# Sums of squares for the first norm from the transposed tiles of x, and x in rows loaded later

## The chip, the cores and the metric

One core of a Trainium2 chip. The metric is the device time of one execution in microseconds (us). Engines: PE is TensorE (matrix products), ACT is ScalarE, DVE is VectorE, POOL is GpSimd, SP is SyncE, which here only issues loads. An engine works off its own instructions in order; engines wait for one another through semaphores.

## What is computed

Two transformer blocks on 256 tokens of width 2048, in float32. What matters here is the very start, the norm of the input and the first projection:

```python
def rms_norm(x, gain):
    xf = x.astype(jnp.float32)
    y = xf * lax.rsqrt(jnp.mean(xf * xf, axis=-1, keepdims=True) + EPS)
    return (y * gain.astype(jnp.float32)).astype(x.dtype)

def hybrid_mixer(xn, w_in, lb, hgrn_onorm, attn_qnorm, attn_knorm, w_out):
    proj = xn @ w_in
...
h = h + hybrid_mixer(rms_norm(h, norm_mix[l]), w_in[l], ...)
```

The mean over a token's 2048 features is a factor of the token alone. So the kernel multiplies x times gain with the weights at once and applies the factor, called `rstd`, when a product leaves PSUM.

## The kernel before

Everything runs on one core, in float32 products of three terms: each operand is split into a high part `hi` (ACT, line 392 for weights, 1379 for x) and a low part `lo` (DVE, lines 393 and 1380), and PE adds hi x hi, hi x lo and lo x hi (lines 443 to 445). Weights come in chunks of 512 KB into four buffers `raw` (SP, line 382); a chunk holds one or two feature tiles of 128 rows for a block of 512 output columns. There are four buffers each of `hi` and `lo`, so that splits run at most four chunks ahead of PE, and a load waits until DVE has split the chunk four places before.

The first two blocks, called c0 and c1 in the code, share the sixteen feature tiles of x transposed. These arrive with the chunks of weights into two regions `r` (line 1369, from an array that the host transposed) and are split by `first_split` into `xT`. The order of chunks at the start is written out by hand: features 0, 1, 2, 3, (4,5), (6,7) in turns for c0 and c1, then (8,9), (10,11), (12,13), (14,15) of c0, and then the same four of c1. A chunk of two tiles is 12 matmuls of 128x512 on PE.

x in rows, the tile `X`, is needed for two things. The residual add at the mixer's end reads it, and so does the sum of squares: `build_ss` (line 308) has ACT square a 128x512 piece with an accumulator (`junk`, the sums go to `ss`), and `make_rstd` adds the four partial sums, scales them and takes the reciprocal root by `rsqrt` (line 246): two integer steps on DVE (`rg`) and twelve small steps on POOL (`rh`, `rstd`). `X` is loaded in four column pieces of 512 KB from POOL's queue, each held back by a copy of eight columns (`gate`) from the low part of feature 5, 7, 9 or 11 (`X_GATES`). `prep` then spreads `rstd` over a row: DVE copies it wide into `wA`, PE transposes twice into `sdA`, DVE copies the result into `rstd_bc` (lines 635 to 647). Then POOL loads a table (`levels`).

What comes when on each engine is set by a planner inside the code. Chunks are emitted in the order above; between two chunks the side work, kept as generators in six lanes, takes a step if a lane's clock says that its data are there. `wait_for` and `mark` carry those estimates. The planner's costs set the order of instructions, and the chip then runs them with real semaphores.

Of the kernel before, what the change touches and what calls it, by code (L numbers as in the profile page):

```python
# [12 lines left out]
F32 = mybir.dt.float32  # L13
# [4 lines left out]
AF = mybir.ActivationFunctionType  # L18
ALU = mybir.AluOpType
# [3 lines left out]
P = 128  # L23
T = 256
D = 2048
KT = D // P
# [3 lines left out]
EPS = 1e-6  # L30
# [16 lines left out]
FIRST_SINGLE = 4  # L47
FIRST_LEN = 10
TURNS = 6
X_GATES = (5, 7, 9, 11)  # L50
WARM_UP = 10
BEHIND = 2.0

# [33 lines left out]
def block_kernel(ctx: ExitStack, tc: "_tile.TileContext", a: dict, out: bass.AP, phases=ALL_PHASES):  # L87
    nc = tc.nc
    ctx.enter_context(tc.manual_schedule())

    const = ctx.enter_context(tc.tile_pool(name="const", bufs=1))
# [7 lines left out]
    ready = {}  # L99
    uid = [0]  # L100

    def nm(s):
        uid[0] += 1
        return f"{s}_{uid[0]}"

    def wt(lane, dtype=F32):
        return tmp.tile([P, 512], dtype, tag=f"w{lane}", bufs={"B": 2, "E": 4, "A": 6}[lane], name=nm(f"w{lane}"))

    def st(role, n=8, dtype=F32):
        return small.tile([P, n], dtype, tag=role, name=nm(role))  # L110

    def sd(lane):
        return ps_side.tile([P, 512], F32, tag=f"sd{lane}", name=nm(f"sd{lane}"))

    def region(i, shape, dtype=F32):
        return reg.tile(shape, dtype, tag=f"r{i}", name=nm(f"r{i}"))
# [5 lines left out]
    clock = {"pe": 0.0, "act": 0.0, "dve": 0.0, "pool": 0.0}  # L122
    names = ("E", "B", "C", "D", "H", "A")
    lanes = {k: deque() for k in names}
# [20 lines left out]
    class Paced:  # L145
# [26 lines left out]
    pe, sca, vec, gps = (  # L172
        Paced(t, e) for t, e in ((nc.tensor, "pe"), (nc.scalar, "act"), (nc.vector, "dve"), (nc.gpsimd, "pool")))

    def mark(key):
        lane = now["lane"]
        ready.setdefault(key, done[lane] if lane is not None else 0.0)
# [37 lines left out]
    def wait_for(*keys):  # L215
        while any(k not in ready for k in keys) or (
            not now["forced"] and max(ready[k] for k in keys) > clock["pe"]
        ):
            yield WAIT
        lane = now["lane"]  # L220
        done[lane] = max([done[lane]] + [ready[k] for k in keys])
        last_on[lane] = None
# [14 lines left out]
    def load_x(c0, c1):  # L237
        nc.gpsimd.dma_start(out=X[:, :, c0:c1], in_=a["x"][:, c0:c1].rearrange("(t p) c -> p t c", p=P))
# [3 lines left out]
    def gcol(i):  # L242
        return gT[:, i : i + 1]


    def rsqrt(lane, x, n, mul=1.0, out=None):

        g = st(f"rg{lane}", n, I32)
        vec.tensor_scalar(g, x.bitcast(I32), 1, None, op0=ALU.logical_shift_right)
        vec.tensor_scalar(g, g, -1, RSQRT_MAGIC, op0=ALU.mult, op1=ALU.add)  # L250
        y = st(f"ry{lane}", n) if out is None else out
        h = st(f"rh{lane}", n)
        for i in range(3):
            y0 = g.bitcast(F32) if i == 0 else y
            m = mul if i == 2 else 1.0
            gps.tensor_tensor(h, y0, y0, op=ALU.mult)
            gps.tensor_tensor(h, h, x, op=ALU.mult)
            gps.tensor_scalar(h, h, -0.5 * m, 1.5 * m, op0=ALU.mult, op1=ALU.add)
            gps.tensor_tensor(y, h, y0, op=ALU.mult)
        return y  # L260

    rstd = {}
    rstd_sq = {}

    def make_rstd(lane, key, ss, want_sq=False):

        v = vec
        m = st(f"mr{lane}", 2)
        v.tensor_reduce(m, ss.rearrange("p (t c) -> p t c", t=2), axis=AX.X, op=ALU.add)
        ms = const.tile([P, 2], F32, name=nm("ms"))  # L270
        v.tensor_scalar(ms, m, 1.0 / D, EPS, op0=ALU.mult, op1=ALU.add)
        if want_sq:
            r2 = const.tile([P, 2], F32, name=nm("rsq"))
            v.reciprocal(r2, ms)
            rstd_sq[key] = r2
        else:
            rstd[key] = rsqrt(lane, ms, 2, out=const.tile([P, 2], F32, name=nm("rstd")))
        mark(("rstd", key))
# [3 lines left out]
    def parts_of(ver, kt):  # L282

        xT = xTs[0 if ver in ("mlp1", "mlp2") else 1]
        return xT[:, kt, 0, :], xT[:, kt, 1, :], xT[:, kt, :, :].rearrange("p x t -> p (x t)")
# [22 lines left out]
    def build_ss(ver, cb, want_sq):  # L308
        yield from wait_for(("x", ver, cb))
        if ver not in ss_tiles:  # L310
            ss_tiles[ver] = const.tile([P, 8], F32, name=nm("ss"))
        ss = ss_tiles[ver]
        for tt in range(2):
            junk = tmp.tile([P, 512], BF16, tag="junk", bufs=1, name=nm("junk"))
            sca.activation(
                junk, X[:, tt, cb * 512 : (cb + 1) * 512], AF.Square,
                accum_out=ss[:, tt * 4 + cb : tt * 4 + cb + 1],
            )
        yield
        if cb == 3:  # L320
            make_rstd("D", ver, ss, want_sq)
            yield
# [7 lines left out]
    acts = {k: Act() for k in ("mix", "cross", "mlp1", "na", "mlp2")}  # L330
# [57 lines left out]
    def emit_split(c):  # L388
        n = len(c.kts) * c.block.width
        c.hi = stream.tile([P, 1024], F32R, tag="hi", name=nm("hi"))  # L390
        c.lo = stream.tile([P, 1024], F32R, tag="lo", name=nm("lo"))
        nc.scalar.activation(c.hi[:, :n], c.raw[:, :n], AF.Copy)  # L392
        nc.vector.tensor_tensor(c.lo[:, :n], c.raw[:, :n], c.hi[:, :n], op=ALU.subtract)  # L393
        clock["act"] = max(clock["act"], clock["pe"] - 2.6) + 0.1 + n * 0.00083
        clock["dve"] = max(clock["dve"], clock["act"] + HOP) + 0.1 + n * 0.00104
        c.ready = clock["dve"]
# [966 lines left out]
    p0 = order[0]  # L1363
    xr = [region(i, [P, 8, T]) for i in (6, 7)]
# [9 lines left out]
    def first_split(kt):  # L1374

        act = acts[p0]
        act.put(kt, *parts_of(p0, kt))
        (hi, lo, _), src, g = act.parts_of[kt], xr[kt // 8][:, kt % 8, :], gcol(gains_of[p0] + kt)
        nc.scalar.activation(hi, src, AF.Copy, scale=g)
        nc.vector.scalar_tensor_tensor(lo, src, g, hi.bitcast(F32), op0=ALU.mult, op1=ALU.subtract)  # L1380
        mark(("act", id(act), kt))

    starters = {
        "mix": mixer, "cross": cross, "mlp1": lambda: mlp("mlp1", a["w_up"], a["w_down"]),
# [1 line left out]
    }  # L1386
    for p_ in order:
        starters[p_]()

    n = len(plan)  # L1390
    dma_i = split_i = 0
# [16 lines left out]
    def split(c):  # L1408
        if c.block.act is acts[p0]:
            for kt in c.kts:  # L1410
                if kt not in made:
                    made.add(kt)
                    first_split(kt)
                    if kt in X_GATES:
                        cb = X_GATES.index(kt)
                        gate = st("gate", 8)
                        nc.gpsimd.tensor_copy(gate, acts[p0].parts[kt][1][:, :8].bitcast(F32))
                        load_x(cb * 512, cb * 512 + 512)
                        ready["x", p0, cb] = clock["pe"] + 10.0
                        lanes["D"].append(build_ss(p0, cb, p0 in ("mlp1", "mlp2")))  # L1420
        emit_split(c)

    while dma_i < RAW_BUFS:
# [2 lines left out]
    while split_i < 2:  # L1426
        split(plan[split_i])
        split_i += 1
    for i in range(n):
        while dma_i < min(n, i + DMA_AHEAD):  # L1430
            while split_i <= dma_i - RAW_BUFS:
                split(plan[split_i])
                split_i += 1
            dma(plan[dma_i])
            dma_i += 1
        while split_i < min(n, i + 1 + SPLIT_AHEAD):
            split(plan[split_i])
            split_i += 1
        emit_mm(plan[i])
        step_all()  # L1440
# [69 lines left out]
```

## Time and profile before

| | us |
|---|---|
| median of 3 runs | 2430.24 (2428.49 to 2430.58) |
| the profiled execution | 2430.18 |
| its span, first to last instruction | 2428.4 |
| PE busy | 2419.5 |
| DVE busy | 1498.1 |
| ACT busy | 1183.2 |
| POOL busy | 183.6 |

The span is that of the profiled execution; 1.8 us of its time lie around the span. All positions in the text are microseconds from the span's start. "Granted clock" is TensorE's clock as a share of full speed. A row of the timeline with "x2" merges two instructions that follow each other, and its duration is that of both together. A float32 product of two plain operands leaves two records on PE.

### The profile page before, as it was taken

Reading aid. Unit: us, or ns where it says so; the run is one execution under the profiler, and the core shown is the slowest. Engines: PE = TensorE matmul, PEld = TensorE weight load, DVE = VectorE, ACT = ScalarE, POOL = GpSimd, SP = SyncE. Lnnn points to the kernel's source line nnn. Section 1 sums busy time; section 2 is a strip of 40 time slices with the busy share of each in tenths; the row PEclk is TensorE's granted clock in tenths of the full one; section 3 lists DMA queues with packets and bytes.
Section 4 is the critical chain, followed back from the end, with each engine's and each line's share of the span. In section 5 each row is a group of like instructions: output and inputs, shape, how many; then the busy total and the mean of one; then the engine's idle time right before and its main releaser. Section 6 shows DMA issues by size and latency. Waiting matters only on the chain.

```text
span 2428.4 us, 32811 instructions
## 1 busy us (share of the span) xinstructions
PE 2419.5 (100%) x12664; PEld 2073.9 (85%) x12664; DVE 1498.1 (62%) x1859; ACT 1183.2 (49%) x1608; POOL 183.6 (8%) x362
## 2 busy tenths in 40 slices
PE   9999999999999999999999999999999999999999
PEld 7979988888888888888888888888888888888887
DVE  6567666666665655565555666776655555655565
ACT  6455544465654444444445454554654444444442
POOL 1021012221000000000000412230000000000000
PEclk9999999999999999999999999999999999999999
DMA  8655444754555655565665655565555665656564
GB/s 283 195 170 170 138 141 158 241 184 157 182 192 190 192 189 188 193 198 184 191 192 181 203 173 179 174 194 177 173 193 185 196 195 187 195 186 192 189 200 164
DMA packets 127292, 453.33 MB, mean 187 GB/s; under 512 B 14608, under 2 KB 15376, under 8 KB 127136
## 3 DMA queue, kind: packets, MB, share of 16 engines
q1 hardware_dynamic: 122688, 439.87, 56.3%
q0 software_dynamic: 3584, 10.00, 1.4%
q8 instruction: 99, 1.62, 0.3%
q10 hardware_dynamic: 864, 1.38, 0.2%
q14 instruction: 57, 0.47, 0.1%
HBM read 449.02 MB, written 2.10 MB: 186 GB/s over the span
## 4 chain that ended last, share of the span: by engine, by line
PE 99%; DMA 0%; DVE 0%; ACT 0%; SPq 0%; issue 0%; ACTq 0%; DVEq 0%
PE acc L424 20%; PE acc L443 20%; PE acc L444 20%; PE acc L445 20%; PE acc L427 10%; PE acc L436 4%; PE sdA L168 3%; PE sdE L168 2%; DMA raw<-in_w_in_dram 0%; DVE lo L393 0%; ACT hi L392 0%; ACT r L168 0%; SPq L1369 0%; DVE X L168 0%; DVE lb L168 0%
## 5 line engine op out<-in xcount | busy, mean ns | idle before, releaser
L393 DVE TENSOR_TENSOR lo<-raw,hi 128x1024 fp32r<-128x1024 f32 (+1 forms) x838 | 1008.8, 1218 | 332.1 <-ACT hi L392 329.4
L392 ACT ACTIVATE hi<-raw 128x1024 fp32r<-128x1024 f32 (+1 forms) x838 | 869.6, 1052 | 552.8 <-PE acc L445 403.5
L424 PE MATMUL acc<-xT,hi 128*128 128x512 f32 (+1 forms) x2176 | 750.7, 391 | 0.0
L427 PE MATMUL acc<-xT,lo 128*128 128x256 f32 (+1 forms) x2176 | 606.2, 279 | 0.0
L443 PE MATMUL acc<-hi,r 128*128 128x512 f32 (+1 forms) x1408 | 543.4, 386 | 0.7 <-ACT r L168 0.7
L445 PE MATMUL acc<-hi,r 128*128 128x512 f32 (+1 forms) x1408 | 541.3, 384 | 0.0
L444 PE MATMUL acc<-lo,r 128*128 128x512 f32 (+1 forms) x1408 | 541.2, 384 | 0.0
L424 PEld LDWEIGHTS acc<-xT,hi 128*128 128x128 f32 x2176 | 408.4, 188 | 88.1
L427 PEld LDWEIGHTS acc<-xT,lo 128*128 128x128 f32 x2176 | 409.7, 188 | 0.6
L445 PEld LDWEIGHTS acc<-hi,r 128*128 128x128 f32 x1408 | 264.5, 188 | 53.1 <-DVE r L168 0.4
L443 PEld LDWEIGHTS acc<-hi,r 128*128 128x128 f32 x1408 | 264.6, 188 | 52.9 <-ACT r L168 1.1
L444 PEld LDWEIGHTS acc<-lo,r 128*128 128x128 f32 x1408 | 264.6, 188 | 51.2
L443 PE MATMUL acc<-hi,xT 128*128 128x512 f32 x736 | 291.6, 396 | 1.2 <-ACT hi L392 1.2
L444 PE MATMUL acc<-lo,xT 128*128 128x512 f32 x736 | 287.7, 391 | 0.8 <-DVE lo L393 0.8
L445 PE MATMUL acc<-hi,xT 128*128 128x512 f32 x736 | 287.2, 390 | 0.0
L168 DVE TENSOR_TENSOR wE<-acc,wE 128x256 f32<-128x256 f32 (+1 forms) x136 | 51.9, 421 | 220.3 <-ACT wE L168 220.2
L168 DVE SCALAR_TENSOR_TENSOR X<-acc,rsq,X 128x512 f32<-128x512 f32 x128 | 96.1, 751 | 147.6 <-PE acc L445 147.6
L168 ACT ACTIVATE wE<-acc 128x256 f32<-128x256 f32 (+1 forms) x136 | 49.3, 381 | 277.3 <-PE acc L427 277.3
L443 PEld LDWEIGHTS acc<-hi,xT 128*128 128x128 f32 x736 | 138.6, 188 | 31.4 <-issue 2.7
L445 PEld LDWEIGHTS acc<-hi,xT 128*128 128x128 f32 x736 | 138.6, 188 | 29.2
L444 PEld LDWEIGHTS acc<-lo,xT 128*128 128x128 f32 x736 | 138.8, 189 | 28.5 <-DVE lo L393 1.5
L436 PE MATMUL acc<-xT,hi 128*128 128x256 f32 (+1 forms) x544 | 100.1, 286 | 0.0
(188 smaller groups left out, 1397.2 us busy)
## 6 DMA issues: line engine op xcount, KB each, us to landing
raw<-in_mlp_w_dram SPq DMA_DIRECT2D x256, 512.0 KB, 4.4
raw<-in_w_up_dram SPq DMA_DIRECT2D x128, 512.0 KB, 4.5
raw<-in_w_down_dram SPq DMA_DIRECT2D x128, 512.0 KB, 4.3
raw<-in_w_in_dram SPq DMA_DIRECT2D x108, 512.0 KB, 3.7
raw<-in_na_w_qkv_dram SPq DMA_DIRECT2D x96, 512.0 KB, 3.7
raw<-in_w_out_dram SPq DMA_DIRECT2D x32, 512.0 KB, 4.3
raw<-in_na_w_o_dram SPq DMA_DIRECT2D x32, 512.0 KB, 3.7
raw<-in_w_iq_dram SPq DMA_DIRECT2D x16, 512.0 KB, 4.8
```

Source lines behind the costliest of these rows:

```text
L168: return f(*args, **kw)
L392: nc.scalar.activation(c.hi[:, :n], c.raw[:, :n], AF.Copy)
L393: nc.vector.tensor_tensor(c.lo[:, :n], c.raw[:, :n], c.hi[:, :n], op=ALU.subtract)
L424: nc.tensor.matmul(dst[:, : 2 * m].rearrange("p (x t) -> p x t", x=2), wh[:, ot : ot + P], both, start=first, stop=False)
L427: nc.tensor.matmul(dst[:, :m], wl[:, ot : ot + P], xh[:, b.t0 :], start=False, stop=last)
L436: nc.tensor.matmul(dst, l, r, start=first and i == 0 and o == 0, stop=last and i == 2, skip_group_check=True,)
L443: nc.tensor.matmul(dst, h, wh, start=first, stop=False)
L444: nc.tensor.matmul(dst, h, wl, start=False, stop=False)
L445: nc.tensor.matmul(dst, l, wh, start=False, stop=last)
```

## The change

The sums of squares come from `r`, the transposed tiles, where a token's features lie across partitions and tiles. ACT squares two tiles at a time (128x512), DVE adds the squares up over the eight pairs (`total`), adds the two halves, and two matmuls with a tile of ones add over the partitions; the result has tokens on partitions again, as `rsqrt` wants it. `build_ss` is no longer used for this first norm (later norms keep it). X is loaded in one go, behind one gate copy from feature tile 15, the last. The work stands in lane D from the start.

```diff
-X_GATES = (5, 7, 9, 11)
...
         mark(("act", id(act), kt))
+        ready["act", id(act), kt] = clock["act"]
+
+    def first_norms():
+
+        ones, total, sq = wt("A"), wt("A"), wt("A")
+        nc.gpsimd.memset(ones[:, :8], 1.0)
+        for k in range(0, KT, 2):
+            yield from wait_for(("act", id(acts[p0]), k), ("act", id(acts[p0]), k + 1))
+            src = xr[k // 8][:, k % 8 : k % 8 + 2, :].rearrange("p k t -> p (k t)")
+            sca.activation(sq if k else total, src, AF.Square)
+            if k:
+                vec.tensor_tensor(total, total, sq, op=ALU.add)
+            yield
+        vec.tensor_tensor(total[:, :T], total[:, :T], total[:, T:], op=ALU.add)
+        yield
+        ps = sd("A")
+        for tt in range(2):
+            pe.matmul(
+                ps[:, tt * 8 : tt * 8 + 8], total[:, tt * P : (tt + 1) * P], ones[:, :8], start=True, stop=True)
+        yield
+        ms = const.tile([P, 2], F32, name=nm("ms"))
+        vec.tensor_scalar(
+            ms, ps[:, :16].rearrange("p (t c) -> p t c", t=2)[:, :, 0], 1.0 / D, EPS, op0=ALU.mult, op1=ALU.add)
+        rstd[p0] = rsqrt("D", ms, 2, out=const.tile([P, 2], F32, name=nm("rstd")))
+        mark(("rstd", p0))
+        yield
...
+    lanes["D"].append(first_norms())
...
                     first_split(kt)
-                    if kt in X_GATES:
-                        cb = X_GATES.index(kt)
+                    if kt == KT - 1:
                         gate = st("gate", 8)
                         nc.gpsimd.tensor_copy(gate, acts[p0].parts[kt][1][:, :8].bitcast(F32))
-                        load_x(cb * 512, cb * 512 + 512)
-                        ready["x", p0, cb] = clock["pe"] + 10.0
-                        lanes["D"].append(build_ss(p0, cb, p0 in ("mlp1", "mlp2")))
+                        for cb in range(4):
+                            load_x(cb * 512, cb * 512 + 512)
```

In the rows below and in the profile, the changed kernel's line numbers are one lower up to the end of `first_split`, and 25 higher behind it at the gate and the loads; helper operations stand at line 167 instead of 168.

On PE, the order of the kernel before from the last matmuls of c1's chunk (12,13) on: the two transposes that spread `rstd` (`sdA`, from `wA`) stand there, ahead of c1's last chunk (14,15).

```order
L444 MATMUL acc_174<-lo_485,xT 128x512
L445 MATMUL acc_174<-hi_484,xT 128x512
L168 MATMUL sdA_541<-cst,wA_520 128x128 x2
L443 MATMUL acc_173<-hi_502,xT 128x512
L444 MATMUL acc_173<-lo_503,xT 128x512
```

On PE, the order of the change, at two places: the two matmuls with ones (`sdA` from two `wA`) between c0's chunks (10,11) and (12,13), and the two transposes behind c0's chunk (14,15), ahead of c1's chunk (8,9).

```order
L443 MATMUL acc_147<-lo_350,xT 128x512
L444 MATMUL acc_147<-hi_349,xT 128x512
L167 MATMUL sdA_422<-wA_154,wA_155 128x8 x2
L442 MATMUL acc_146<-hi_373,xT 128x512
L443 MATMUL acc_146<-lo_374,xT 128x512
...
L443 MATMUL acc_147<-lo_404,xT 128x512
L444 MATMUL acc_147<-hi_403,xT 128x512
L167 MATMUL sdA_485<-cst,wA_482 128x128 x2
L442 MATMUL acc_178<-hi_446,xT 128x512
L443 MATMUL acc_178<-lo_447,xT 128x512
```

The transposes moved forward past three chunks of c1, 36 matmuls, and the ones stand 24 matmuls ahead of them. From the first chunk of the third block on, PE's order is the same in both.

On DVE, the order of the change from the split of c0's chunk (12,13) on; `wA_155` is `total`, `ms` reads the ones' result, `rgD` are the integer steps of the root, and `wA_482` is the wide copy of `rstd`.

```order
L392 TENSOR_TENSOR lo_374<-raw_318,hi_373 128x1024
L167 TENSOR_TENSOR wA_155<-wA_155,wA_156 128x512
L1379 SCALAR_TENSOR_TENSOR xT<-r_5_102,cst,xT 128x256 x2
L392 TENSOR_TENSOR lo_404<-raw_343,hi_403 128x1024
L167 TENSOR_TENSOR wA_155<-wA_155,wA_156 128x512
L167 TENSOR_TENSOR wA_155<-wA_155 128x256
L167 TENSOR_SCALAR ms_425<-sdA_422 128x2
L167 TENSOR_SCALAR rgD_428<-ms_425 128x2
L167 TENSOR_SCALAR rgD_428<-rgD_428 128x2
L392 TENSOR_TENSOR lo_447<-raw_367,hi_446 128x1024
L392 TENSOR_TENSOR lo_465<-raw_391,hi_464 128x1024
L167 COPY wA_482<-rstd_427 128x128 x2
```

Before, the reduce of `ss` and the scale stood behind the splits of c1's chunks (8,9) and (10,11), two chunks later. On POOL four loads of `X` now stand in a row behind the one gate copy, directly ahead of the root's steps:

```order
L1386 MEMSET wA_154 128x8
L1442 COPY gate_397<-xT 128x8
L237 DMA X<-in_x_dram 128x2x512 x4
L167 ISA
L167 TENSOR_TENSOR rhD_431<-rgD_428 128x2
```

Before, each load followed a gate copy of its own, among the splits of features 5 to 11.

## Rows read from the trace of the kernel before

**Rows 1.** The page: busy time, and the chain that ended last by engine.
```profile
PE 2419.5 (100%) x12664; PEld 2073.9 (85%) x12664; DVE 1498.1 (62%) x1859; ACT 1183.2 (49%) x1608; POOL 183.6 (8%) x362
...
PE 99%; DMA 0%; DVE 0%; ACT 0%; SPq 0%; issue 0%; ACTq 0%; DVEq 0%
```

**Rows 2.** Waits of PE: us in total, times, longest; the largest after the start.
```profile
PE acc L443 <- ACT hi L392: 1.2, 1, 1.2
```

**Rows 3.** Timeline of PE around the waits: start us, us, instruction, idle before.
```profile
16.95 0.39 PE L445 MATMUL acc<-hi,xT 128*128 128x512 f32 x1
...
18.58 0.51 PE L443 MATMUL acc<-hi,xT 128*128 128x512 f32 x1 [1.24 <-ACT hi L392]
...
19.83 0.80 PE L444 MATMUL acc<-lo,xT 128*128 128x512 f32 x1 [0.75 <-DVE lo L393]
...
23.20 0.40 PE L443 MATMUL acc<-hi,xT 128*128 128x512 f32 x1
...
37.27 0.39 PE L445 MATMUL acc<-hi,xT 128*128 128x512 f32 x1
```

**Rows 4.** Stretches: length, busy (PE, PEld, DVE, ACT, POOL), clock, DMA share, GB/s.
```profile
19.90:22.90 3.00, 3.00 (x7) 2.41 (x8) 2.77 (x4) 1.78 (x3) 0.61 (x2) 0.50 1.06 393
```

**Rows 5.** POOL's load queue, 14:19.9, then 19.9:36.3 us: packets, MB, share.
```profile
q0 software_dynamic: 1, 0.00, 0.2%
...
q0 software_dynamic: 563, 2.06, 32.5%
```

**Rows 6.** Timeline of POOL: loads of X, a gate copy, root steps.
```profile
15.86 0.73 POOL L238 DMA_DIRECT2D X<-in_x_dram  x1
...
22.48 0.72 POOL L238 DMA_DIRECT2D X<-in_x_dram  x1 [0.28 <-issue]
26.96 1.15 POOL L1417 COPY gate<-xT 128x8 f32<-128x8 f32 x1 [3.76 <-DVE xT L1380]
...
42.58 1.10 POOL L168 TENSOR_TENSOR rhD<-rgD 128x2 f32<-128x2 f32 x1 [11.77 <-DVE rgD L168]
...
44.31 1.19 POOL L168 TENSOR_TENSOR rstd<-rhD,rgD 128x2 f32<-128x2 f32 x1
...
47.52 0.20 POOL L168 TENSOR_TENSOR rstd<-rhD,rstd 128x2 f32<-128x2 f32 x1
```

**Rows 7.** Tile X up to 120 us: ACT's squares, ns min/median/max.
```profile
L168 ACT ACTIVATE junk<-X x8: 614/632/634, 26.7 to 38.9; 128x512 bf16<-128x512 f32 x8
L168 ACT ACTIVATION_READ_ACCUMULATOR junk<-X x8: 186/187/188, 27.2 to 39.4; 128x1 f32 x8
```

**Rows 8.** Timeline of DVE: splits, scale, wide copies of rstd.
```profile
12.29 0.69 DVE L393 TENSOR_TENSOR lo<-raw,hi 128x512 fp32r<-128x512 f32 x1
...
18.55 2.52 DVE L393 TENSOR_TENSOR lo<-raw,hi 128x1024 fp32r<-128x1024 f32 x2 [2.89 <-ACT hi L392]
20.99 0.88 DVE L1380 SCALAR_TENSOR_TENSOR xT<-r,cst,xT 128x256 fp32r<-128x256 f32 x2
22.10 1.23 DVE L393 TENSOR_TENSOR lo<-raw,hi 128x1024 fp32r<-128x1024 f32 x1 [0.23 <-ACT hi L392]
...
41.92 0.17 DVE L168 TENSOR_SCALAR ms<-mrD 128x2 f32<-128x2 f32 x1
...
47.75 0.36 DVE L168 COPY wA<-rstd 128x128 f32<-128x128 f32 x2 [2.29 <-POOL rstd L168]
51.51 0.42 DVE L168 COPY rstd_bc<-sdA 128x256 f32<-128x256 f32 x1 [0.29 <-PE sdA L168]
```

**Rows 9.** Timeline of PE: the two transposes, and later narrow f32 matmuls.
```profile
51.10 0.38 PE L168 MATMUL sdA<-cst,wA 128*128 128x128 f32 x2
...
269.49 1.90 PE L168 MATMUL sdE<-r,r 128*128 128x64 f32 x16
271.19 0.48 PE L436 MATMUL acc<-xT,hi 128*128 128x256 f32 x2
```

**Rows 10.** Timeline of POOL: loads in a row, in the stage with the memory.
```profile
453.99 1.19 POOL L1136 DMA_DIRECT2D wA<-in_memt_dram  x2
```

## The prediction

> **What bounds the kernel now.** I read the page first: TensorE (PE) is busy for 2419.5 of 2428.4 us, and 99% of the chain that ended last is PE [rows 1]. So a microsecond counts only where PE waits, where its clock falls, or where it gets more to do. The list of PE's waits comes next: beside the start, the largest is 1.2 us for a high part `hi` [rows 2], and the next, 0.75 us, is for the low part `lo` of the same chunk [rows 3]. Both lie in the stretch that this change edits. By the timeline the last undisturbed matmul starts at 16.95, the next at 18.58, then 19.83, and the tenth after 16.95 at 23.20 [rows 3]. From 23.20 to 37.27 there are 62 matmuls, 0.227 us apart; at that spacing the tenth would have stood at 19.22, so this place costs 4.0 us. The stretch table shows the rest of it: after the two waits the granted clock is 0.50 from 19.9 to 22.9 us, the 1.2 GHz level of the two [rows 4]. That row also has the DMA engines fully busy, at 393 GB/s, and it is tempting to blame the 2 MB of x in rows. The queues decide that: up to 19.9 us the queue that carries x moved 1 of its packets, and from 19.9 to 36.3 us 563, 2.06 MB [rows 5]. The first load of x was issued at 15.86 [rows 6], but its bytes came when the wait was over. So moving x cannot shorten the wait; what it frees lies between 20 and 36 us, where PE does not wait. That is why I forecast no gain from the change's main part.
>
> **What goes.** On ACT, eight squares of 0.63 us with accumulator reads of 0.19 us [rows 7], 6.6 us in all, on DVE one small reduce, on POOL three of four gate copies. All of it lies beside PE: worth nothing by itself.
>
> **What is added.** On ACT eight squares of the same 128x512 shape without accumulator reads, 5.0 us by the same row [rows 7]. On DVE seven 128x512 adds of two SBUF inputs; the nearest row is the split of that shape, 0.69 us alone [rows 8], I take 0.65 in a row, and 0.42 for the last, 128x256 add, as a copy of 256 columns takes [rows 8]: 5.0 us. Bounds for one add: 0.4 to 0.75 us. They are hidden as long as the splits stay ahead of PE. Count DVE from 18.55 [rows 8] until the last add: 8 splits of 1.2, 5 pairs of feature splits of 0.85, 6 adds of 0.65 and 0.42 make 18.2 us, so it ends at 36.7 if DVE never starves. ACT has 1.6 us less to do than before, when it was in time. In this count the split of (12,13) ends near 33 and that of (14,15) near 35.6, against 37.5 and 40.2 where PE wants them.
>
> **Where PE meets it.** By the order, the two matmuls with ones stand on PE behind the chunk of features (10,11), two chunks ahead of (14,15) whose squares they need. PE is there at 37.27 + 0.23 = 37.5 [rows 3]; the last add is done at 36.7. So PE does not wait at this place, by 0.8 us. It pays for the two matmuls: float32 products leave two records each, and the nearest narrow ones, 16 records of 64 columns, push the next matmul from 269.49 to 271.19 [rows 9], 0.11 us a record. Four records: **0.43 us** (bounds 0.2, half of it, to 0.6 with a broken weight prefetch). PE goes on at 37.93.
>
> **Where PE waits next.** `rstd` must come out before the two transposes that spread it, and these now stand only two chunks, 24 matmuls, behind the ones: PE is there at 37.93 + 24 x 0.227 = 43.4. Before, it was there at 51.10 [rows 9], while the copies that it needs ran at 47.75 [rows 8], some 3 us of slack. Now the chain is: the result of the ones in PSUM near 38.1, the scale on DVE, 0.66 us later POOL's first step (41.92 to 42.58 before [rows 6, 8]), 12 POOL steps from 42.58 to 47.72 [rows 6], which is 5.14 us, then copies of 0.36 us [rows 8]. That is 38.1 + 0.66 + 5.14 = 43.9, and 44.3 for both copies: PE waits **0.9 us**. The 5.14 us hold two steps of 1.1 and 1.2 us where others take 0.2; I keep both, since two splits follow on DVE right behind the scale here too. Without them the chain is 3.3 us, and PE waits for nothing; with one more such step it waits 1.8 us.
>
> **POOL's queue.** The four loads of x now go out in a row ahead of that chain. The gate copy waits for the split of feature 15, near 34.4, and can take 1.15 us beside DVE [rows 6]; four issues of 0.72 us end near 38.5. DVE has the scale ready for POOL at 38.8. So this just fits, with 0.3 us to spare. A load's issue took 0.72 us even at 22.48, beside the split that ran on DVE from 22.10 [rows 6, 8], and loads follow each other without a gap in the later stage with the memory [rows 10].
>
> The Trainium skill has a rule against this placement (SBUF — State Buffer, section "SBUF: two separate sides"): a transfer issued from GpSimd has its descriptors written by GpSimd, and these wait while VectorE holds the port pair that the two share. By that rule each issue would wait for a split, and the sum would be 4.5 us more; by the row at 22.48 it is 0.
>
> **Behind it.** `rstd` comes near 44 instead of 47.7, and ACT's evacuation of the first block, then the split of c1's third remaining chunk, are queued behind it on ACT; PE wants that split near 50, and has it near 47.5. x lands near 45, its first reader is the residual add of the mixer, several hundred us later: nothing. Behind the first 200 matmuls the order of PE is the old one, and so nothing comes back later.
>
> **Sum.** 0.43 + 0.9 = 1.3 us slower, in a profiled run of 2430.18 us (span 2428.4 and 1.8 around it), which stands 0.06 us under the median of 2430.24. **2431.5 us.** Its own bounds: 0.2 + 0 to 0.6 + 1.8, and 1.5 us more if the clock falls again as it did after the waits at 17 to 20 us (half of the 3.0 us at 0.50 [rows 4]): 2430.4 to 2434.1.
>
> **Rivals.**
> - *The early wait shrinks.* If some of the loads of x did slow the chunk that PE waited for, up to 4.0 us come back: 2430.2 + 1.3 - 4.0 = 2427.5. Against it: 1 packet before 19.9 us [rows 5]. Chance 0.10.
> - *The ones come too early for DVE.* If a late landing or slower adds let the last add end past 37.5, PE waits at the ones for the difference, with the rest as before. One us late gives 2432.5. For it: only 0.8 us of slack, worked out from single durations. Chance 0.12.
> - *POOL is the bound (slower).* The loads of x hold POOL longer than their issue rows say. x's bytes came 4 us after its issue (15.86 to 19.9); if POOL were held that long for each, it would be free at 35.6 + 16 = 51.6 instead of 38.8, and the transposes with it: 12.8 us more, 2444. It decides from POOL free at 42.3 on, where the sum passes 0.2%. Against it: the loads back to back [rows 10]. Chance 0.08.
> - *Each issue waits for DVE.* Four issues, each longer by a split of 1.2 us: POOL is free at 38.5 + 4.8 = 43.3, 4.5 us after 38.8, which gives 2436. For it: the gate copy at 26.96, which did take 1.15 us [rows 6]. This is the mechanism of the page named above. Chance 0.06.
> - *Nothing is paid.* POOL's steps run free of DVE, and only the ones cost: 2430.5. Chance 0.14.
>
> **How the numbers follow.** My forecast has the remaining 0.50. 0.2% is 4.9 us, about what a measurement of this kernel can tell from no change; forecast, no cost, early ones and most of the gain lie within it. Slower by over that: POOL as the bound, most of the waiting issues, and a forecast with everything at its end: 0.12. Faster by over that would need more than the whole 4.0 us that stand there: 0.02. Same: 0.86. The runs before spread over 2428.49 to 2430.58, so the low end is 2428.5, and the high end takes in the waiting issues: 2436.5.
>
> **What would show it.** Right: the waits at 17 to 20 us and the clock of 0.50 unchanged; a new PE wait below 1.5 us at the transposes near 43.4, for DVE's copy of `rstd`; no wait at the ones near 37.5; ACT without accumulator reads; x's packets from about 39 us. Wrong: no wait of over 0.5 us at 17 us; a wait at the ones; POOL's first step of the root past 40 us, or PE waiting at the transposes for several us.

## The result: slower by 21 us, and the profile after

The changed kernel takes 2451.53 us (median of 4 runs, 2450.31 to 2452.18) beside 2430.14 for the kernel before (4 runs, 2428.49 to 2430.58): ratio 1.009, 95% interval 1.0078 to 1.0102. The profiled run took 2452.06 us, span 2450.3. The forecast was 2431.5 with a range up to 2436.5, so it was wrong, by some 20 us.

The page of the changed kernel, the rows that answer to [rows 1]:
```profile
PE 2441.4 (100%) x12668; PEld 2075.7 (85%) x12668; DVE 1502.0 (61%) x1866; ACT 1182.3 (48%) x1600; POOL 182.7 (7%) x360
...
PE 99%; DMA 0%; DVE 0%; POOL 0%; ACT 0%; issue 0%; SPq 0%; ACTq 0%; DVEq 0%
```
PE is busy for 21.9 us more, with four records more. The time did not go into a wait, and the list of PE's waits says so too; this answers to [rows 2]:
```profile
PE acc L442 <- ACT hi L391: 1.0, 1, 1.0
...
PE sdA L167 <- DVE wA L167: 0.3, 1, 0.3
```
The second row is the new wait at the two transposes. Nothing else in the list is new by more than 0.2 us. L442 to L444 here are L443 to L445 of before, and L423 is L424.

**The start.** PE's timeline, beside [rows 3, 9]:
```profile
18.55 0.50 PE L442 MATMUL acc<-hi,xT 128*128 128x512 f32 x1 [0.96 <-ACT hi L391]
...
19.81 0.50 PE L443 MATMUL acc<-lo,xT 128*128 128x512 f32 x1 [0.76 <-DVE lo L392]
...
38.02 0.51 PE L167 MATMUL sdA<-wA,wA 128*128 128x8 f32 x4
38.39 0.47 PE L442 MATMUL acc<-hi,xT 128*128 128x512 f32 x1
38.70 0.39 PE L443 MATMUL acc<-lo,xT 128*128 128x512 f32 x1
...
43.83 0.40 PE L444 MATMUL acc<-hi,xT 128*128 128x512 f32 x1
44.54 0.47 PE L167 MATMUL sdA<-cst,wA 128*128 128x128 f32 x2 [0.32 <-DVE wA L167]
```
The two waits are where they were, the ones come without a wait, the transposes with a short one. But from 38.70 to 43.83 there are 22 steps of one matmul, 0.233 us each, where the kernel before has 0.227 from 23.20 to 37.27 [rows 3]. The stretch table after the early waits, beside [rows 4]:
```profile
20.00:23.00 3.00, 3.00 (x8) 2.34 (x8) 3.00 (x5) 3.00 (x5) 0.00 (x0) 0.54 0.93 328
```
The granted clock is down here, as it was. POOL, beside [rows 6]:
```profile
33.61 0.19 POOL L1442 COPY gate<-xT 128x8 f32<-128x8 f32 x1 [31.04 <-DVE xT L1379]
33.74 2.84 POOL L237 DMA_DIRECT2D X<-in_x_dram  x4
39.22 1.10 POOL L167 TENSOR_TENSOR rhD<-rgD 128x2 f32<-128x2 f32 x1 [2.64 <-DVE rgD L167]
...
44.03 0.20 POOL L167 TENSOR_TENSOR rstd<-rhD,rstd 128x2 f32<-128x2 f32 x1
```
And DVE, beside [rows 8]:
```profile
33.72 1.23 DVE L392 TENSOR_TENSOR lo<-raw,hi 128x1024 fp32r<-128x1024 f32 x1 [0.18 <-ACT hi L391]
34.86 0.68 DVE L167 TENSOR_TENSOR wA<-wA,wA 128x512 f32<-128x512 f32 x1
35.58 0.42 DVE L167 TENSOR_TENSOR wA<-wA 128x256 f32<-128x256 f32 x1
38.57 0.16 DVE L167 TENSOR_SCALAR ms<-sdA 128x2 f32<-128x2 f32 x1 [2.56 <-PE sdA L167]
...
44.26 0.36 DVE L167 COPY wA<-rstd 128x128 f32<-128x128 f32 x2 [2.85 <-POOL rstd L167]
```

**Where the 21 us are.** SP issues the weight loads in the same order in both kernels, each when a buffer of `raw` comes free, so its timeline tells how far a kernel has come. The kernel before, at the first load of four stages (mlp1, na, its output product, and one of the last loads):
```profile
602.26 0.33 SPq L382 DMA_DIRECT2D raw<-in_w_up_dram  x1
...
1314.55 1.46 SPq L382 DMA_DIRECT2D raw<-in_na_w_qkv_dram  x2
...
1603.39 0.33 SPq L382 DMA_DIRECT2D raw<-in_na_w_o_dram  x1
...
2402.21 0.89 SPq L382 DMA_DIRECT2D raw<-in_mlp_w_dram  x2
```
The changed kernel at the same loads:
```profile
606.98 0.33 SPq L381 DMA_DIRECT2D raw<-in_w_up_dram  x1
...
1324.49 1.47 SPq L381 DMA_DIRECT2D raw<-in_na_w_qkv_dram  x2
...
1619.45 0.33 SPq L381 DMA_DIRECT2D raw<-in_na_w_o_dram  x1
...
2424.05 0.89 SPq L381 DMA_DIRECT2D raw<-in_mlp_w_dram  x2
```
The lag is 4.7 us at 602, 9.9 at 1315, 16.1 at 1603 and 21.8 at the end. It grows over the whole kernel, in code that the change does not touch. The page's costliest groups say in which instructions; the kernel before (busy us, mean ns):
```profile
L424 PE MATMUL acc<-xT,hi 128*128 128x512 f32 (+1 forms) x2176 | 750.7, 391 | 0.0
L443 PE MATMUL acc<-hi,r 128*128 128x512 f32 (+1 forms) x1408 | 543.4, 386 | 0.7 <-ACT r L168 0.7
...
L443 PE MATMUL acc<-hi,xT 128*128 128x512 f32 x736 | 291.6, 396 | 1.2 <-ACT hi L392 1.2
L444 PE MATMUL acc<-lo,xT 128*128 128x512 f32 x736 | 287.7, 391 | 0.8 <-DVE lo L393 0.8
L445 PE MATMUL acc<-hi,xT 128*128 128x512 f32 x736 | 287.2, 390 | 0.0
```
The changed kernel:
```profile
L423 PE MATMUL acc<-xT,hi 128*128 128x512 f32 (+1 forms) x2176 | 761.1, 396 | 0.0
...
L442 PE MATMUL acc<-hi,r 128*128 128x512 f32 (+1 forms) x1408 | 543.7, 386 | 0.7 <-ACT r L167 0.7
...
L442 PE MATMUL acc<-hi,xT 128*128 128x512 f32 x736 | 296.3, 403 | 1.0 <-ACT hi L391 1.0
L443 PE MATMUL acc<-lo,xT 128*128 128x512 f32 x736 | 291.8, 396 | 0.8 <-DVE lo L392 0.8
L444 PE MATMUL acc<-hi,xT 128*128 128x512 f32 x736 | 291.5, 396 | 0.0
```
The matmuls of 512 columns between `xT` and the split weights got slower by 5 to 7 ns each: +10.4 us in the first row, +4.7, +4.1 and +4.3 in the last three, 23.5 in all; one row of narrower matmuls (L436 of before, 256 columns) got 2.1 us faster. Those between `r` and the same weights did not change.

**Two theories.** *Addresses:* the first norm no longer makes its tile `ss`, 32 bytes in each partition of SBUF, which stood ahead of the weight buffers. By the list of allocations of the two built programs, the tiles behind it, from the weight buffers to the regions, start 32 bytes lower: the first `hi` at 89088 instead of 89120, a region `r` at 138240 instead of 138272. `xT` stayed at 34816. So `hi` and `lo` moved against `xT`, and `r` moved with them. *The changed start (rival):* later loads of x, or a shifted phase of the streams, disturb PE throughout.

### The profile page after: what moved, and what is told of

Read it like the earlier page. It is cut to its first block, busy times and chain, and to the rows that moved or that the text cites. A ratio compares the mean times of both kernels' runs of the same rounds, so it can differ in the third digit from the quotient of the medians.

```text
span 2450.3 us, 32811 instructions
## 1 busy us (share of the span) xinstructions
PE 2441.4 (100%) x12668; PEld 2075.7 (85%) x12668; DVE 1502.0 (61%) x1866; ACT 1182.3 (48%) x1600; POOL 182.7 (7%) x360
## 4 chain that ended last, share of the span: by engine, by line
PE 99%; DMA 0%; DVE 0%; POOL 0%; ACT 0%; issue 0%; SPq 0%; ACTq 0%; DVEq 0%
PE acc L423 21%; PE acc L442 20%; PE acc L444 20%; PE acc L443 20%; PE acc L426 10%; PE acc L435 4%; PE sdA L167 3%; PE sdE L167 2%; DMA raw<-in_w_in_dram 0%; POOL rhD L167 0%; DVE lo L392 0%; ACT hi L391 0%; ACT r L167 0%; SPq L1368 0%; DVE X L167 0%
## 5 line engine op out<-in xcount | busy, mean ns | idle before, releaser
L423 PE MATMUL acc<-xT,hi 128*128 128x512 f32 (+1 forms) x2176 | 761.1, 396 | 0.0
L442 PE MATMUL acc<-hi,r 128*128 128x512 f32 (+1 forms) x1408 | 543.7, 386 | 0.7 <-ACT r L167 0.7
L444 PE MATMUL acc<-hi,r 128*128 128x512 f32 (+1 forms) x1408 | 541.5, 385 | 0.0
L443 PE MATMUL acc<-lo,r 128*128 128x512 f32 (+1 forms) x1408 | 541.3, 384 | 0.0
L423 PEld LDWEIGHTS acc<-xT,hi 128*128 128x128 f32 x2176 | 408.8, 188 | 95.7
L444 PEld LDWEIGHTS acc<-hi,r 128*128 128x128 f32 x1408 | 264.5, 188 | 53.4 <-DVE r L167 0.4
L442 PEld LDWEIGHTS acc<-hi,r 128*128 128x128 f32 x1408 | 264.6, 188 | 52.9 <-ACT r L167 1.1
L443 PEld LDWEIGHTS acc<-lo,r 128*128 128x128 f32 x1408 | 264.7, 188 | 51.2
L442 PE MATMUL acc<-hi,xT 128*128 128x512 f32 x736 | 296.3, 403 | 1.0 <-ACT hi L391 1.0
L443 PE MATMUL acc<-lo,xT 128*128 128x512 f32 x736 | 291.8, 396 | 0.8 <-DVE lo L392 0.8
L444 PE MATMUL acc<-hi,xT 128*128 128x512 f32 x736 | 291.5, 396 | 0.0
L442 PEld LDWEIGHTS acc<-hi,xT 128*128 128x128 f32 x736 | 138.9, 189 | 34.8 <-issue 2.7
L444 PEld LDWEIGHTS acc<-hi,xT 128*128 128x128 f32 x736 | 138.8, 189 | 33.4
L443 PEld LDWEIGHTS acc<-lo,xT 128*128 128x128 f32 x736 | 139.0, 189 | 32.0 <-DVE lo L392 1.1
```

What stands on the lines that cost most here:

```text
L423: nc.tensor.matmul(dst[:, : 2 * m].rearrange("p (x t) -> p x t", x=2), wh[:, ot : ot + P], both, start=first, stop=False)
L442: nc.tensor.matmul(dst, h, wh, start=first, stop=False)
L443: nc.tensor.matmul(dst, h, wl, start=False, stop=False)
L444: nc.tensor.matmul(dst, l, wh, start=False, stop=last)
```

## The experiments

Three forms of matmul are told apart. In the **wide** form (mlp1 and mlp2, L424 of before) `hi` is the stationary operand and both halves of `xT`, 512 columns, move. In the **normal** form (L443 to L445; mix, cross, na) 128 tokens of `xT` are stationary and 512 columns of `hi` or `lo` move; the **r form** is the same with `r` in the place of `xT`. By the kernel's `for o in (0, 8)`, `xT` starts at 34816 in the mlps and 32 bytes later in the other stages.

This table was worked out from the matmul records of each trace: ns from a matmul's start to the next one's, the mean for the wide form (2048 of 512 columns), the median for the others (first of the three lines). The columns ahead of it are the start of each operand in bytes modulo 64 (a + means another 64 bytes up); "us" is the median of the runs.
```
kernel                     xT:mlp  xT:others  hi   r    wide   normal  r     us
before                     0       32         32   32   230.6  227     227   2430.1
changed                    0       32         0    0    236.4  235     227   2451.5
 1 changed, 32 unused      0       32         32   32   230.8  227     227   2431.6
 2 before, ss moved        0       32         0    0    236.6  234     227   2449.3
 3 changed, xT exchanged   32      0          0    0    228.8  227     227   2428.8
 4 changed, xT 32 in       32      32         0    0    228.8  234     227   2437.1
 5 before, as 3            32      0          0    0    228.6  227     227   2427.1
 6 3 again                 32      0          0    0    228.6  227     227   2427.4
 7 changed, 64 unused      0       32         0+   0+   235.1  234     227   2453.1
 8 before, r alone moved   0       32         32   0    234.7  227     235   2464.3
 9 before, xT exchanged    32      0          32   32   235.7  234     227   2450.1
10 changed, 96 unused      0       32         32+  32+  229.4  230     227   2426.9
11 before, 64 unused       0       32         32+  32+  229.4  229     227   2425.9
12 5, 64 unused            32      0          0+   0+   230.6  231     227   2429.5
```

### 1. The changed kernel with the 32 bytes put back

```diff
+        const.tile([P, 8], F32, name="pad")
         ones, total, sq = wt("A"), wt("A"), wt("A")
```


> The changed kernel with one unused tile of 32 bytes a partition put back where the first norm's ss stood, so that every tile behind it (raw, hi, lo, the regions) has the address that it had in the kernel before. Address theory: the matmuls of xT with hi go back to 229 and 227 ns from start to start (median; the changed kernel has 236 and 233 to 235), the lag behind the kernel before stays at the start's 1 to 1.5 us, and the time is 2431 to 2432 us. Rival theory (the changed start itself, its later x loads or the shifted phase of the streams, slows PE): the time stays at 2451 us and the spacing at 233 to 236 ns.

2431.61 us (2430.80 to 2432.97), ratio to before 1.0009 (1.0000 to 1.0019). The page has the old durations back:
```profile
L423 PE MATMUL acc<-xT,hi 128*128 128x512 f32 (+1 forms) x2176 | 750.7, 391 | 0.0
...
L442 PE MATMUL acc<-hi,xT 128*128 128x512 f32 x736 | 291.6, 396 | 0.5 <-ACT hi L391 0.5
```
One unused tile takes 20 of the 21 us away, with the whole change in place. The rival falls for these 20.

### 2. The kernel before with its ss moved away

```diff
-            ss_tiles[ver] = const.tile([P, 8], F32, name=nm("ss"))
+            ss_tiles[ver] = (st("ss0") if not ss_tiles else const.tile([P, 8], F32, name=nm("ss")))
```


> The kernel before with nothing changed but the place of the first norm's ss, which goes to the end of SBUF, so that every tile behind it moves down by 32 bytes to the addresses of the changed kernel. Address theory: 2449 to 2451 us, all of it by xT with hi matmuls at 233 to 236 ns, without any part of the change. Rival theory (the changed start): 2430 us, no difference.

2449.31 us, ratio 1.0084 (1.0069 to 1.0099), by the same groups:
```profile
L424 PE MATMUL acc<-xT,hi 128*128 128x512 f32 (+1 forms) x2176 | 761.1, 397 | 0.0
...
L443 PE MATMUL acc<-hi,xT 128*128 128x512 f32 x736 | 295.8, 402 | 0.1
```
The loss comes without any part of the change. (The change also reorders some work tiles behind the regions; here they keep the old order, so that the loss does not hang on it.)

### 3. The changed kernel with the two starts of xT exchanged

```diff
-    xTs = [xTt[:, o : o + KT * 2 * T].rearrange("p (k x t) -> p k x t", k=KT, x=2) for o in (0, 8)]
+    xTs = [xTt[:, o : o + KT * 2 * T].rearrange("p (k x t) -> p k x t", k=KT, x=2) for o in (8, 0)]
```


> The changed kernel with the two starts of xT exchanged: 0 for mix, cross and na, 32 bytes for mlp1 and mlp2. If the place of hi relative to xT decides: both forms change their distance by 32 bytes and the time goes back to 2431 to 2433 us. If hi's own address decides whatever xT's is: both forms stay slow and the time stays at 2451 us. If only xT's own address decides, the wide form alone or the other form alone changes, by about 10 us each.

2428.84 us, ratio 0.9996 (0.9987 to 1.0006): all of the loss is gone, and `hi` is where the changed kernel has it. So `hi`'s address by itself does not decide, and how the two operands lie to each other can; number 9 shows the same from the other side. It came out 2 us below the expectation, by the wide form (228.8 ns where number 1 has 230.8):
```profile
L423 PE MATMUL acc<-xT,hi 128*128 128x512 f32 (+1 forms) x2176 | 747.7, 389 | 0.0
...
L442 PE MATMUL acc<-hi,xT 128*128 128x512 f32 x736 | 291.4, 396 | 1.3 <-ACT hi L391 1.2
```

### 4. The changed kernel with xT 32 bytes in for every stage

```diff
-    xTs = [xTt[:, o : o + KT * 2 * T].rearrange("p (k x t) -> p k x t", k=KT, x=2) for o in (0, 8)]
+    xTs = [xTt[:, o : o + KT * 2 * T].rearrange("p (k x t) -> p k x t", k=KT, x=2) for o in (8, 8)]
```


> The changed kernel with xT starting 32 bytes in for every stage, which changes mlp1 and mlp2 alone. If the place of hi relative to xT decides: the wide form (2048 matmuls) gets its 6 to 7 ns back and the time is 2440 to 2442 us, with mix, cross and na as slow as in the changed kernel. If hi's own address decides: 2451 us.

2437.09 us (ratio 1.0036, 1.0023 to 1.0049). The forms separate: the wide one is cured, the normal one as slow as in the changed kernel. The time is 3 us under the expectation for the same reason as in 3.
```profile
L423 PE MATMUL acc<-xT,hi 128*128 128x512 f32 (+1 forms) x2176 | 748.0, 389 | 0.0
...
L442 PE MATMUL acc<-hi,xT 128*128 128x512 f32 x736 | 295.5, 401 | 0.8 <-ACT hi L391 0.8
```

### 5 and 6. The addresses of 3, without the change and with it

Number 5 is number 2 with the line of number 3; number 6 is number 3 once more, in the same rounds. ("The last run but one of the changed kernel" in the first text is number 3.)

> The kernel before, with the first norm's ss at the end of SBUF (hi, lo and the regions 32 bytes lower, as in the changed kernel) and the starts of xT exchanged (0 for mix, cross and na, 32 bytes for mlp1 and mlp2): the addresses of the last run but one of the changed kernel, without the change. Address theory with the distance deciding: the wide form at 228.8 ns where the kernel before has 230.6 (2048 x 1.8 ns = 3.7 us less) and the rest unchanged: 2426 us, faster than both kernels. If the gain of the exchanged kernel came from the changed start: 2430 us.

> The changed kernel with the starts of xT exchanged, once more, on the chip and in the rounds of the kernel above, which differs from it by the change alone. The prediction's sum for the change alone was +1.3 us: 2427 to 2428 us beside 2426. If the change alone costs nothing: the same time as the kernel above; if its start costs more than the sum said: 3 us or more above it.

2427.12 us without the change (ratio 0.9988, 0.9979 to 0.9997) and 2427.37 with it (0.9992, 0.9983 to 1.0001). Number 5 is faster than both kernels. Its 11 runs and the 11 of number 6 each fall into two sets by their mean granted clock, 1.000 or 0.999; set against set, the change costs 2427.19 - 2425.76 = 1.4 us (7 and 5 runs) and 2428.97 - 2427.41 = 1.6 us (4 and 6 runs). That is the term that the prediction put at 1.3.

### 7 and 10. The changed kernel with 64 and with 96 unused bytes

As number 1, with `[P, 16]` and `[P, 24]`.

> The changed kernel with an unused tile of 64 bytes in the place of ss, so that everything behind it stands 64 bytes higher than in the changed kernel and 32 bytes higher than before. If the distance of hi and xT counts in steps of 32 bytes within 64: as the changed kernel, 2451 us, with 236 and 233 to 235 ns. If the changed kernel was slow for being below the old address, or if a longer step (128 bytes or more) decides: another time, 2430 us if any move upwards is free.

> The changed kernel with 96 unused bytes in the place of ss, everything behind it 64 bytes above the kernel before. If the distance counts within 64 bytes: as with 32 unused bytes, 2431 to 2432 us. If 128 bytes or more count: another time, towards 2451 us.

64 bytes: 2453.08 us (ratio 1.0097, 1.0083 to 1.0111), as slow as the changed kernel, so that the loss is no matter of standing lower than before. 96 bytes: 2426.86 us (0.9990, 0.9980 to 1.0000): fast again, as steps of 32 within 64 say, but 4.8 us under number 1 (4.6 by their ratios to before, each taken in rounds of its own), where the same time was expected. Part of that is the wide form (229.4 ns for 230.8), part a narrow one, which takes 98.0 us in the changed kernel and 100.1 in number 1:
```profile
L435 PE MATMUL acc<-xT,hi 128*128 128x256 f32 (+1 forms) x544 | 96.4, 281 | 0.0
```
So 64 bytes more have an effect of their own, a quarter as large.

### 8. The kernel before with r alone moved

```diff
     ready = {}
     uid = [0]
+    reg.tile([P, 8], F32, tag="pad", name="pad")
```


> The kernel before with 32 unused bytes ahead of the regions r, so that r moves by 32 bytes against hi while hi against xT stays. If the matmuls of hi and lo with r (4224 of them at 227 ns) follow the same rule as those with xT: 6 to 7 ns each, 25 to 30 us more, 2456 to 2460 us. If the rule is one of xT alone: 2430 us.

2464.34 us, ratio 1.0145 (1.0131 to 1.0159): a tile of 32 bytes that nothing reads or writes costs 34 us.
```profile
L425 PE MATMUL acc<-xT,hi 128*128 128x512 f32 (+1 forms) x2176 | 761.0, 395 | 0.0
L444 PE MATMUL acc<-hi,r 128*128 128x512 f32 (+1 forms) x1408 | 551.6, 392 | 0.7 <-ACT r L169 0.7
...
L444 PE MATMUL acc<-hi,xT 128*128 128x512 f32 x736 | 290.9, 395 | 0.9 <-ACT hi L393 0.9
```
The r form, spared in the changed kernel because `r` had moved with `hi`, pays 8.2 us a line here, some 25 us for its three lines. The first row was not expected: the wide form, whose operands had not moved, pays 10 us too (below). The work tiles behind `r` moved with it.

### 9. The kernel before with the starts of xT exchanged

The line of number 3, in the kernel before.

> The kernel before with the starts of xT exchanged (0 for mix, cross and na, 32 bytes for mlp1 and mlp2) and everything else where it was. If the distance of the two operands decides, this is wrong for both forms, as in the changed kernel: xT with hi at 232 to 236 ns, 2449 to 2452 us. If the exchanged starts are good by themselves (hi's place does not matter): 2426 us.

2450.08 us, ratio 1.0083 (1.0068 to 1.0098): the exchange that cures the changed kernel costs the old one as much.
```profile
L424 PE MATMUL acc<-xT,hi 128*128 128x512 f32 (+1 forms) x2176 | 759.6, 395 | 0.0
...
L443 PE MATMUL acc<-hi,xT 128*128 128x512 f32 x736 | 294.8, 401 | 1.4 <-ACT hi L392 1.4
```

### 11 and 12. Another 64 bytes without the change

In number 11 the kernel before has an unused `[P, 16]` tile ahead of `ss`, in number 12 number 5 has one at the same place.

> The kernel before with 64 unused bytes ahead of ss, so that hi, lo and the regions stand where they stood in the changed kernel with 96 unused bytes. If the 4.8 us between 96 and 32 unused bytes are the address alone: 2425.4 us (2426.9 less the 1.5 us of the change itself). If 64 bytes do nothing and that run was an accident: 2430 us.

> The kernel before with xT's starts exchanged and ss at the end, as in the fastest kernel so far, and with 64 unused bytes ahead of hi. If the distance within 64 bytes is all: 2427 us, as there. If another 64 bytes matter as they did between 32 and 96 unused bytes: up to 5 us either way, 2422 to 2432 us.

Number 11: 2425.89 us, ratio 0.9984 (0.9975 to 0.9993), the fastest of all, and 1.0 us under number 10, which is the same with the change (1.5 by the ratios). Number 12: 2429.45 us (1.0000, 0.9991 to 1.0009), 2.3 above number 5 (2.9 by the ratios). The 64 bytes gain at one place of `xT` and lose at the other.

## Why the prediction was wrong, step by step

**The step that failed** is the sentence under "Behind it": "Behind the first 200 matmuls the order of PE is the old one, and so nothing comes back later." The order is indeed the old one. The operands are not where they were, and with the same order the matmuls of the normal form take 233 to 235 ns for 227 and those of the wide form 236 for 231. That is 20 of the 21 us; numbers 1 and 2 show it from both sides. "What goes" counted the instructions that vanish and not the tile that vanishes with them. No rival had it either, so the range had no place for it.

**No gain from moving x: right.** The early waits are 0.96 and 0.76 us beside 1.24 and 0.75 [rows 3], and x's queue moved nothing from 14 to 33 us; its first packets came between 33 and 36 us, not from about 39 as said. The low clock behind these waits held in the changed kernel (0.54 from 20 to 23 us) and is no property of the kernel: numbers 1 to 4 and 8 to 12 have 1.00 there, numbers 5 to 7 have 0.53 to 0.60. The 1.5 us that the bounds kept for a fall of the clock behind the new wait were not needed: it is 1.00 from 38 to 60 us.

**What is added: right.** The squares take 0.614 us (5.0 us were given for eight, it is 4.9), an add 0.68 where 0.65 was taken, the last add 0.42 as taken. It ends at 36.0; 36.7 was said.

**The ones: right.** They came at 38.02 without a wait (37.5 said), and pushed the next matmuls from 38.02 to 38.47 (38.70 less one step of 0.23): 0.45 us for 0.43. The slack was thin: in number 3, where PE was there at 35.9, it waited 0.2 us for the last add.

**The transposes: right in size, in part by luck.** POOL's root ran from 39.22 to 44.23, 5.0 us for 5.14, with the two long steps that were kept; PE, itself later there, waited 0.5 us. Number 1, which has the old addresses, on PE, POOL and DVE:
```profile
41.14 0.39 PE L444 MATMUL acc<-hi,xT 128*128 128x512 f32 x1
42.25 0.46 PE L167 MATMUL sdA<-cst,wA 128*128 128x128 f32 x2 [0.72 <-DVE wA L167]
...
33.05 1.72 POOL L1443 COPY gate<-xT 128x8 f32<-128x8 f32 x1 [30.49 <-DVE xT L1379]
34.73 2.84 POOL L237 DMA_DIRECT2D X<-in_x_dram  x4
37.68 1.22 POOL L167 TENSOR_TENSOR rhD<-rgD 128x2 f32<-128x2 f32 x1
...
36.41 0.45 DVE L167 TENSOR_SCALAR rgD<-rgD 128x2 int32<-128x2 int32 x1
```
The last matmul ahead of the transposes started at 41.14, so their turn was at 41.37, and they started at 42.25: 0.9 us, as forecast. But two errors cancel in it. DVE had the root's input ready at 36.86, and POOL began 0.8 us later (in the changed kernel 0.1 us later), straight from the fourth load; the root then took 4.25 us, with one long step instead of two.

**POOL's queue: no fixed margin.** In the profiled run of the changed kernel the gate copy took 0.19 us and not 1.15, and POOL was free at 36.6 instead of 38.5. In number 1 it took 1.72 us. There, and in numbers 3, 4 and 10, POOL was still issuing loads when DVE was ready, and the root began 0.8 to 1.2 us behind DVE. So POOL did become the bound there, the rival's case in small; at equal addresses the change still costs no more than some 2 us (below).

None of the issues waited for DVE: the four took 2.84 us in a row, 0.70 to 0.73 each, while DVE ran a split from 33.72 and an add from 34.86. The prediction stretched the rule of the Trainium skill (SBUF — State Buffer, "SBUF: two separate sides") here: by that section an operation of VectorE with two SBUF inputs, as splits and adds are, shuts out only a GpSimd operation that reads SBUF. The traces agree: what took long reads SBUF, the gate copy in number 1 (1.72 us, beside a split and an add) and the first two steps of the root (1.10 and 1.06 us, beside the splits of 39.05), and the issues did not.

**The sum** of 1.3 us for what was counted stands: at equal addresses the change costs 2.2 us in number 1 against before, 0.25 in 6 against 5 (1.4 to 1.6 at equal clock), 1.0 in 10 against 11. All lie within the 0.2% that a measurement can tell, so the total agrees with the sum, but it cannot prove the sum's terms.

## What to carry to other kernels

"The instruction order is unchanged" does not mean that the instructions take as long as before: a tile that a change adds or drops in a bump-allocated pool moves everything behind it (such a pool hands out addresses one after the other). Where PE is the bound and the same operands meet thousands of times, compare the start addresses of the operands before and after, modulo 64 bytes, as well as the order, and hold them with an unused tile; code that already places a tile 8 floats in, as `xT` here, may be a sign that somebody met this. Measure a change at equal addresses before judging its idea: this one costs some 1 to 2 us, and the 20 us come from the tile that it dropped, not from its idea.

## What the runs showed that was not expected

- **Operands that lie apart.** In the normal and the r form, 512 columns of `hi` or `lo` that move against a stationary `xT` or `r` take 227 ns (up to 231 in 10 to 12) where the starts are equal modulo 64 bytes, and 232 to 235 where they are 32 apart. Every row of the table agrees on this, with `xT` alone moved (3, 9), `r` without `hi` (8), and `hi`, `lo` and `r` together (2). In the wide form it is the other way round: 229 to 231 ns where the starts differ by 32 (but for number 8, below), and 235 to 237 where they are equal. Why the two forms want opposite things the runs do not tell, and it stays open.
- **A pattern that a stretch keeps.** In number 8 the wide form's operands lie as before, yet its matmuls take 229 and 240 ns in turn, 63 of each 128 at 240. The kernel before has that pattern too, in the first 256 matmuls of each mlp (124 and 120 at 240) and in none of the later stretches of 128. Numbers 1 and 12 have it in the same places, numbers 3 to 6, 10 and 11 nowhere, and it is most of what tells their 230.6 to 230.8 ns from 228.6 to 229.4. So the addresses of a form's own operands are not all of it. Either how the matmuls ahead leave the engine or, in number 8, the tiles behind `r` that moved with it may decide which pattern a stretch falls into; neither was tried.
- **The granted clock at the start.** The half-speed stretch from 20 to 23 us comes in some executions of a kernel and not in others: numbers 3 and 6 are one kernel, with 1.00 there in one trace and 0.56 in the other. Of the fourteen traces, the five with it have a mean clock of 0.999 and the nine without it 1.000. In the kernel before, 21 runs beside numbers 5 to 8 make 9 with a mean clock of 0.999, median 2430.49 us, and 12 with 1.000, median 2429.15. If the mean clock tells here too which runs had the stretch, this is much of the scatter of the times, and as large as the term that the prediction worked out.
